# The mixer's front of a decoder layer: its matmuls, vector and scalar work put in a written order, and the branch weights split into parts during the gates

## The chip, the cores and the metric

The kernel runs on one core of a Trainium2 chip. The metric is the device time of one execution in microseconds. A core has a matrix engine (TensorE, PE in the profile), a vector engine (VectorE, DVE), a scalar engine (ScalarE, ACT), a general engine (GpSimd, POOL) and an engine that here only issues transfers (SyncE, SP). Each of them takes its own instructions strictly in order and waits for the others by semaphores.

## The reference

One layer of a decoder trunk, batch 1, 1024 positions of width 1024, all in f32:

```python
x = x + 0.5 * swiglu(rmsnorm(x), ffn1)
z = rmsnorm(x) @ w_in                  # u | v | c_q | c_kv | k_rope | q_mem | three gates
u, v = gelu(z_u), gelu(z_v)
y_a = spatial_gating(u, v)             # u * (tril(W) layernorm(v) + b), chunks of 128, 8 groups
y_b = mla(c_q, c_kv, k_rope)           # 8 heads, causal, latent queries and keys (w_uq, w_ukv)
y_c = memory_attention(q_mem, mem)     # 4 heads of 128, 256 memory tokens, softmax
gates = sigmoid(z_gates + b)
merged = gates_A * (y_a @ w_a) + gates_B * (y_b @ w_b) + gates_C * (y_c @ w_c)
x = x + merged @ w_out
x = x + 0.5 * swiglu(rmsnorm(x), ffn2)
```

## The kernel before, in words

**Products in three passes.** An f32 operand is split into a high part (a cast, on ScalarE, line 134) and a low part (the operand minus the high part, on VectorE, line 135). A product is three matmuls, high by high, low by high and high by low (`mm3`, lines 148 to 150). Weights that are loaded as f32 go through the same split in `convert`.

**Stages.** First feed-forward half; the input projection (class `Gates`: 19 units of output columns, in a product scheme of Strassen's kind, each of some 19 us); the mixer; output projection; second feed-forward half. The projection leaves u (after GELU), the gates and the latent columns in DRAM tiles named gate, and the memory queries as zhi and zlo; the value columns of z (w_v) are left to the mixer.

**The mixer's front** has four pieces of work, all written in `mixer`:

- Value rows: four groups of two chunks of 128 positions (half f = 1 first, then 0), 48 matmuls each, GELU on ScalarE (line 582), the layer norm on VectorE (statistics line 591, centring 593, the reciprocal root in nine small operations 163 to 167, scaling 596), then a split into tiles h.
- Spatial gating (`gating`): mix(f, j) multiplies a quarter of the groups, ScalarE adds the bias (633); out(f, j) transposes the result on TensorE (643), VectorE multiplies by u (644) and the product is split.
- Memory attention (`mem_attention`): scores(t) for eight blocks of 128 positions into one of two PSUM pairs mm; a minimum on VectorE (724), four exponentials on ScalarE (732) into a tile mpr, of which there are four, the division by the sum (736, 737); turn(i) transposes, value(i) multiplies by the memory values.
- Branch steps (`branches`): y_a @ w_a and later y_c @ w_c. A step takes one tile of 128 output channels, a half of 512 positions, 12 matmuls into one bank; a sink on VectorE multiplies by the gate row (937 for A, 943 for C). A's product is stored in DRAM (md); C's sink loads md, GpSimd adds, and the sum is stored (mc).

Four PSUM banks (`bank`), two pairs (`mm`), five tiles each of whi and wlo, three of raw and six rows t are shared by all of it. In the front before, the framework's scheduler chooses the order of the instructions on each engine, with the order of the code as its first guess; `mixer` uses branch A's steps as filler by calling `next` on the generator.

**Behind the front** stand the latent norm, the query and key/value products of the latent attention (`qkv`), and the attention. There `next` on branch C's generator gives filler: two steps in `mixer`, one in each of the eight blocks of `qkv`, and the rest while the attention gets its first operands. These go through DRAM: q and k are normed on VectorE (lines 516 to 525), stored as qd and kd (533, 530), loaded as aq and ak, half 0 and half 1 (`pair_half`, 543) and transposed on TensorE (406).

SP's queue issues nearly all transfers. A transfer whose tile is not yet free holds up all behind it in the queue.

## Time and profile before

| What | Value |
|---|---|
| Time, median of 3 runs | 2188.55 us (2187.59 to 2189.79) |
| Span of the profiled execution | 2187.2 us, which is 1.35 us below that median |
| PE busy | 2163.2 us, 99% |
| DVE, ACT, POOL busy | 1560.4 us (71%), 908.5 us (42%), 219.0 us (10%) |
| Moved by DMA | 315.80 MB, mean 144 GB/s |

The profiled execution is one run with its own time, and only its span is given. The span is the time from the first to the last instruction of that execution; the runs' times are those of whole executions. The granted clock of TensorE is 0.9 or more in all 40 slices. In the rows, a name such as whi or bank is that of a tile in the program, and L135 is line 135.

Places on the span's axis: the gates end at about 1060 us, the front reaches to about 1150, the last key/value product ends at 1256, and the attention's first transposed operands come at 1272.

### The profile page before, as it was taken

What the parts mean: (1) busy time and instruction counts of PE and PEld (TensorE: products, weight loads), DVE (VectorE), ACT (ScalarE), POOL (GpSimd) and SP (SyncE); (2) the same over time, 40 slices, a digit from 0 to 9 for tenths busy, and PEclk for the clock granted to TensorE, in tenths of its full rate; (3) what the DMA queues carried; (4) which work ended last, traced back from release to release, by engine and by line L of the source; (5) the groups of instructions that cost most, each with busy time, mean ns of one, the idle gap of its engine ahead of it and who ended that gap; (6) DMA issues with size and microseconds to landing.
All of it is one profiled execution on the core that took longest, in us unless ns stands there. A gap on an engine that the chain in (4) does not pass through costs nothing.

```text
span 2187.2 us, 27190 instructions
## 1 busy us (share of the span) xinstructions
PE 2163.2 (99%) x10153; PEld 1797.6 (82%) x10153; DVE 1560.4 (71%) x2285; ACT 908.5 (42%) x1375; POOL 219.0 (10%) x234
## 2 busy tenths in 40 slices
PE   8999999999999999999999999999999999999999
PEld 4788888888888888888888889988888888888887
DVE  7965666569889657556588788898985665556964
ACT  5432223233445435433266549844532322224332
POOL 0011212110000220000000431200001111211000
PEclk9999999999999999999999999999999999999999
DMA  4232333384432673334356661166243333338442
GB/s 155 88 124 91 112 101 114 107 329 151 151 125 81 227 260 106 135 135 170 118 173 198 207 202 35 54 229 238 82 135 96 97 115 92 116 130 317 140 140 97
DMA packets 131925, 315.80 MB, mean 144 GB/s; under 512 B 14608, under 2 KB 23056, under 8 KB 131792
## 3 DMA queue, kind: packets, MB, share of 16 engines
q1 hardware_dynamic: 129392, 311.69, 42.6%
q10 hardware_dynamic: 2400, 2.36, 0.3%
q8 instruction: 80, 1.31, 0.3%
q14 instruction: 53, 0.43, 0.1%
HBM read 216.35 MB, written 97.65 MB: 144 GB/s over the span
## 4 chain that ended last, share of the span: by engine, by line
PE 87%; DVE 9%; DMA 2%; ACT 1%; issue 1%; POOL 0%; SPq 0%; ACTq 0%; DVEq 0%; POOLq 0%
PE one L148 15%; PE one L150 15%; PE one L149 15%; PE bank L148 10%; PE bank L149 10%; PE bank L150 10%; PE mm L148 2%; DVE wlo L135 2%; PE mm L150 2%; PE mm L149 2%; PE bank L864 1%; PE bank L879 1%; DVE h L135 1%; PE bank L880 1%; PE bank L406 1%
## 5 line engine op out<-in xcount | busy, mean ns | idle before, releaser
L134 ACT CAST whi<-x 128x1024 fp32r<-128x1024 f32 (+1 forms) x213 | 200.5, 946 | 510.4 <-PE one L149 213.1
L1457 DVE TENSOR_TENSOR t<-t,one 128x512 f32<-128x512 f32 x149 | 102.3, 687 | 245.0 <-PE one L150 244.8
L135 DVE TENSOR_TENSOR wlo<-x,whi 128x1024 fp32r<-128x1024 f32 (+1 forms) x213 | 233.3, 1099 | 42.5 <-ACT whi L134 42.5
L148 PE MATMUL bank<-h,whi 128*128 128x512 f32 x592 | 231.1, 391 | 1.1 <-ACT t L1483 0.7
L149 PE MATMUL bank<-h,whi 128*128 128x512 f32 x592 | 230.5, 389 | 0.0
L150 PE MATMUL bank<-h,wlo 128*128 128x512 f32 x592 | 230.4, 390 | 0.0
L135 DVE TENSOR_TENSOR wlo<-w,whi 128x1024 fp32r<-128x1024 f32 (+1 forms) x153 | 168.8, 1117 | 75.3 <-ACT whi L134 75.1
L134 ACT CAST whi<-w 128x1024 fp32r<-128x1024 f32 (+1 forms) x153 | 142.4, 954 | 167.0 <-PE one L149 104.9
L148 PE MATMUL one<-h,whi 128*128 128x512 f32 x528 | 206.6, 391 | 1.7 <-ACT t L1483 1.2
L150 PE MATMUL one<-h,wlo 128*128 128x512 f32 x528 | 205.6, 389 | 0.5 <-DVE wlo L135 0.5
L149 PE MATMUL one<-h,whi 128*128 128x512 f32 x528 | 205.5, 389 | 0.0
L148 PE MATMUL one<-w,whi 128*128 128x512 f32 x464 | 180.7, 390 | 0.3 <-DVE t L1457 0.3
L150 PE MATMUL one<-w,wlo 128*128 128x512 f32 x464 | 180.6, 389 | 0.0
L1971 POOL TENSOR_TENSOR raw<-raw 128x512 f32<-128x512 f32 x36 | 75.6, 2100 | 882.5 <-DVE raw L1829 652.2
L1457 DVE TENSOR_TENSOR raw<-t,one 128x512 f32<-128x512 f32 x130 | 89.1, 686 | 88.1 <-PE one L150 81.1
L149 PE MATMUL one<-w,whi 128*128 128x512 f32 x380 | 147.9, 389 | 0.0
L148 PE MATMUL one<-whi 128*128 128x512 f32 (+1 forms) x371 | 143.9, 388 | 0.0
L149 PE MATMUL one<-wlo,whi 128*128 128x512 f32 (+1 forms) x371 | 143.7, 387 | 0.0
L150 PE MATMUL one<-whi,wlo 128*128 128x512 f32 (+1 forms) x371 | 143.7, 387 | 0.0
L148 PEld LDWEIGHTS bank<-h,whi 128*128 128x128 f32 x592 | 111.1, 188 | 24.6 <-ACT t L1483 1.2
L150 PEld LDWEIGHTS bank<-h,wlo 128*128 128x128 f32 x592 | 111.1, 188 | 23.2
L149 PEld LDWEIGHTS bank<-h,whi 128*128 128x128 f32 x592 | 111.2, 188 | 22.7
(424 smaller groups left out, 4784.8 us busy)
## 6 DMA issues: line engine op xcount, KB each, us to landing
x<-in_ffn_w_gu_dram SPq DMA_DIRECT2D x76, 512.0 KB, 4.4
w<-tdt SPq DMA_DIRECT2D x40, 512.0 KB, 3.8
tdb<-raw SPq DMA_DIRECT2D x64, 256.0 KB, 2.0
gate<-raw SPq DMA_DIRECT2D x32, 512.0 KB, 3.5
w<-tdb SPq DMA_DIRECT2D x30, 512.0 KB, 6.9
h<-in_ffn_w_down_dram SPq DMA_DIRECT2D x28, 512.0 KB, 6.5
x<-in_w_in_dram SPq DMA_DIRECT2D x26, 512.0 KB, 6.1
tdt<-w SPq DMA_DIRECT2D x44, 256.0 KB, 2.0
```

What stands on the lines that cost most here:

```text
L134: (copy or self.nc.scalar.copy)(hi, src)
L135: return (eng or self.nc.vector).tensor_tensor(lo, src, hi.bitcast(F32), op=ALU.subtract)
L148: mmul(out, s[0], m[0], start=first, stop=False, **kw)
L149: mmul(out, s[0], m[1], start=False, stop=False, **kw)
L150: self.last = mmul(out, s[1], m[0], start=False, stop=last, **kw)
L406: nc.tensor.transpose(b[:m, k * P:(k + 1) * P], s, self.ident)
L864: nc.tensor.transpose(b[:, at:at + P], prs[t][:, kk * P:(kk + 1) * P], self.ident)
L879: nc.tensor.matmul(o, w, pt[0], start=n == 0, stop=False)
L880: nc.tensor.matmul(o, w, pt[1], start=False, stop=n == len(pts) - 1)
L1457: return self.nc.vector.tensor_tensor(out, x, y, op=ALU.add)
L1971: sub = lambda d, x, y: eng.tensor_tensor(d, x, y, op=ALU.subtract)
```

## The change

**Weights as parts.** `Gates` gets a method `part`. In units 9 to 15 it loads 512 KB of a weight that the mixer will want (branch A and C two tiles at a time, three blocks of w_uq, two of w_ukv: 13 parts), splits it as described and stores both halves in DRAM (wparts). It uses the tiles x4 and w4 of the units' own rings. The mixer then loads ready high and low parts: a branch-A tile into one whi or wlo tile, a branch-C tile into one raw tile, the query and key weights into whi and wlo pairs. No split of these weights is left in the mixer, and twice the bytes are loaded there.

**The written order.** The front runs inside `manual_schedule` for PE, DVE and Activation: on these three engines the instructions stand as the code is written. The helpers are cut into smaller functions (`rows`, `gelu`, `center`, `norm`, `put` for the value rows; `scores`, `exps`, `scale`, `turn`, `value` for the memory attention; `mix` and `out` for the gating), and `mixer` calls them one by one. The scores of blocks 0 to 3 stand inside the value rows; before, all of them came behind. All 16 steps of branch A stand in the front (before, 13), six tiles of half 1 first in place of four. The gate rows of branch A have a ring of their own of two tiles, and a sink stands one step later than its matmuls (lag = 1). mpr has six tiles. Exponentials and GELU now alternate on ScalarE.

The diff, cut to what moves (a line of only "..." marks what is left out; the old `value_rows` and `value_norm` did what `values` does):

```diff
-        wq = self.load(a["mla_w_uq"])
-        wk = [self.load(a["mla_w_ukv"][g]) for g in range(2)]
+        def weights(n, width):
+            t = [self.wide(x, F32)[:, :2 * width].rearrange("p (c w) -> p c w", c=2) for x in ("whi", "wlo")]
+            for i, x in enumerate(t):
+                nc.sync.dma_start(x, self.wparts[n][:, i])
+            return [tuple(x[:, c].bitcast(F32R) for x in t) for c in range(2)]
+
+        wq = [x for q in range(QR // P) for x in weights(("q", q), H * QK // 2)]
+        wk = [weights(("k", g), 512) for g in range(2)]
...
+    def branches(self, br, yt, sink, halves, rooms, first=3, row=None, lag=0):
+
+        nc, w, rooms, held = self.nc, {}, list(rooms), []
 
         steps = [(dt, hf) for hf in halves for dt in range(first)]
         for dt, hf in steps + [(dt, hf) for dt in range(first, DT) for hf in halves]:
             if dt not in w:
-                w[dt] = self.load(
-                    a["w_branch"][br, dt], rooms.pop(0) if rooms else None,
-                    copy=nc.vector.tensor_copy if br == 2 and dt >= DT - 2 else None)
-            sig = self.row()
+                t = rooms.pop(0)()
+                nc.sync.dma_start(
+                    t.rearrange("p (a w) -> p a w", a=2), self.wparts[br, dt // 2][:, :, dt % 2])
+                t = t.bitcast(F32R)
+                w[dt] = [
+                    tuple(t[:, x + k * P:x + (k + 1) * P] for x in (0, 512)) for k in range(4)]
+            sig = (row or self.row)()
             nc.sync.dma_start(sig, self.sig[br * DT + dt][:, hf])
             b = self.bank()
             self.branch(b, w[dt], yt, hf)
-            sink(dt, hf, sig, b)
+            held.append((dt, hf, sig, b))
+            if len(held) > lag:
+                sink(*held.pop(0))
             yield
+        for x in held:
+            sink(*x)
...
-            if d in aside:
-                aside[d]()
...
+    def values(self, h, w, ln_g, ln_b, vs):
+
+        v, groups = self.nc.vector, [(1, 0), (1, 1), (0, 0), (0, 1)]
+        bank, x, mv, out = {}, {}, {}, {}
+
+        def rows(n, d0=0, d1=DT):
+            f, q = groups[n]
+            if n not in bank:
+                bank[n] = [self.bank() for _ in range(2)]
+            for d in range(d0, d1):
+                for i, b in enumerate(bank[n]):
+                    c = slice((2 * q + i) * P, (2 * q + i + 1) * P)
+                    self.mm3(b, tuple(y[:, c] for y in h[f][d]), w[d], d == 0, d == DT - 1)
+
+        def gelu(n):
+            x[n] = self.x4()
+            for k in range(2):
+                self.nc.scalar.activation(x[n][:, k], bank[n][k], ACT.Gelu)
...
-            for t in range(4):
-                scores(t)
-                for go in lead[t]:
-                    go()
-                if t == 1:
-                    query(1)
-            yt += [self.split_pair(self.h4) for _ in range(MH)]
-            for i in range(4):
-                turn(i)
-                fill()
-                if i < 2:
-                    scores(2 * i + 4)
-                if i == 3:
-                    fill()
-                value(i)
-                if i < 3:
-                    fill()
-                if i < 2:
-                    scores(2 * i + 5)
-        return filler
+    def mem_attention(self, p, kt, vv, qt, nr, yt):
+
+        nc = self.nc
+        sc, pr, sm, pt = {}, {}, {}, {}
+
+        def scores(t):
+            sc[t] = self.mm().rearrange("p a (b m) -> p (a b) m", b=2)
+            for hh in range(MH):
+                self.mm3(
+                    sc[t][:, hh], tuple(x[:, t % 4 * P:t % 4 * P + P] for x in qt[hh, t // 4]),
+                    tuple(x[:, hh] for x in kt), True, True)
+
+        def exps(t):
+            mx = self.stat("m_mx", MH)
+            nc.vector.tensor_reduce(mx, sc[t], axis=AXX, op=ALU.min)
+            nc.vector.scalar_tensor_tensor(
+                mx, in0=mx, scalar=-1.0, in1=nr[:, t], op0=ALU.mult, op1=ALU.mult)
+            pr[t] = p.tile([P, MH, ML], F32, name="mpr", bufs=6)
+            sm[t] = self.stat("m_sm", MH)
...
+        E = mybir.EngineType
+        with tc.tile_pool(name="mem", bufs=1) as p, tc.manual_schedule(engines={E.PE, E.DVE, E.Activation}):
             w = self.convert(self.w_v)
             kt, vv = self.mem_operands(p)
             qt, nr, query = self.mem_query(p)
             query(0)
-            vs = [[], []]
-            sw = self.gating_weights()
-            ya, aside = self.gating(sw, vs)
-            branch_a = self.branches(0, ya, sink_a, (1, 0), first=4)
-            fill, mix = (lambda x=x: next(x) for x in (branch_a, aside))
-            for f, q, also in ((1, 0, {}), (1, 1, {}), (0, 0, {}), (0, 1, {d: mix for d in (1, 2, 4, 6, 7)})):
-                x = self.value_rows(f, q, h, w, also)
-                self.value_norm(x, q, ln_g, ln_b, vs[f])
-            lead = [(fill, fill), (fill, mix, mix), (mix, fill), (mix, mix, fill)]
-            branch_c = self.mem_attention(
-                kt, vv, qt, nr, query, lead, branch_a, lambda yc: self.branches(
-                    2, yc, sink_c, (0, 1), [self.half_pair] * DT, first=1))
+            vs, yc = [[], []], []
+            ya, mix, out = self.gating(self.gating_weights(), vs)
+            row = lambda: p.tile([P, 512], F32, name="sig", bufs=2)
+            wide = [lambda x=x: self.wide(x, F32) for x in ("whi", "wlo")]
+            branch_a = self.branches(0, ya, sink_a, (1, 0), wide * (DT // 2), first=6, row=row, lag=1)
+            step = lambda: next(branch_a, None)
+            rows, gelu, center, norm, put = self.values(h, w, ln_g, ln_b, vs)
+            scores, exps, scale, turn, value = self.mem_attention(p, kt, vv, qt, nr, yc)
+
+            rows(0)
+            gelu(0)
+            center(0)
+            norm(0)
+            rows(1, 0, 4)
+            scores(0)
+            exps(0)
+            rows(1, 4)
+            gelu(1)
+            scale(0)
+            put(0)
+            scores(1)
+            exps(1)
+            center(1)
+            norm(1)
+            scale(1)
+            rows(2, 0, 4)
+            scores(2)
+            put(1)
+            exps(2)
+            rows(2, 4)
+            scores(3)
+            scale(2)
+            gelu(2)
+            exps(3)
+            center(2)
+            query(1)
+            rows(3, 0, 2)
+            mix(1, 0)
+            rows(3, 2, 3)
+            mix(1, 1)
+            rows(3, 3, 4)
+            out(1, 0)
+            norm(2)
+            mix(1, 2)
+            rows(3, 4, 5)
+            out(1, 1)
+            mix(1, 3)
+            rows(3, 5, 6)
+            put(2)
+            out(1, 2)
+            scale(3)
+            rows(3, 6, 7)
+            out(1, 3)
+            rows(3, 7)
+            gelu(3)
+            scores(4)
+            exps(4)
+            step()
+            center(3)
+            step()
+            norm(3)
+            step()
+            scale(4)
+            put(3)
+            step()
+            mix(0, 0)
+            mix(0, 1)
+            step()
+            out(0, 0)
+            mix(0, 2)
+            step()
+            out(0, 1)
+            mix(0, 3)
+            scores(5)
+            out(0, 2)
+            exps(5)
+            turn(0, 0)
+            out(0, 3)
+            turn(0, 1)
+            scale(5)
+            step()
+            scores(6)
+            exps(6)
+            step()
+            value(0)
+            scale(6)
+            turn(1, 0)
+            turn(1, 1)
+            step()
+            scores(7)
+            exps(7)
+            step()
+            value(1)
+            scale(7)
+            turn(2, 0)
+            turn(2, 1)
+            step()
+            step()
+            value(2)
+            turn(3, 0)
+            turn(3, 1)
+            step()
+            step()
+            value(3)
+            for _ in range(3):
+                step()
+            branch_c = self.branches(2, yc, sink_c, (0, 1), [self.raw] * DT, first=1)
...
+    def part(self, n, src, a, b):
+
+        k, nc = self.k, self.nc
+        a, b = (t()[:, :, :src.shape[-1]] for t in (a, b))
+        nc.sync.dma_start(a, src)
+        hi, lo = b.bitcast(F32R), a.bitcast(F32R)
+        nc.scalar.copy(hi, a)
+        nc.vector.tensor_tensor(lo, a, b, op=ALU.subtract)
+        for i, t in enumerate((b, a)):
+            nc.sync.dma_start(k.wparts[n][:, i], t)
...
+        k.wparts, parts = {}, []
+        for n, src in chain(
+                (((br, q), k.a["w_branch"][br, 2 * q:2 * q + 2].rearrange("c p k w -> p c (k w)"))
+                 for br in (0, 2) for q in range(DT // 2)),
+                ((("q", q), k.a["mla_w_uq"][:, 2 * q:2 * q + 2]) for q in range(QR // P)),
+                ((("k", g), k.a["mla_w_ukv"][g]) for g in range(2))):
+            k.wparts[n] = k.dram.tile([P, 2, *src.shape[1:]], F32, name=f"wp_{n[0]}{n[1]}")
+            parts.append((n, src))
...
+                if f > MEM_AT:
+                    rooms = list(turn[(last - f + 1) % 2])
+                    while parts and rooms:
+                        self.part(*parts.pop(0), rooms.pop(0), rooms.pop(0))
```

Three places in the instructions' order show how it moves them. First TensorE where the attention gets its first operands; ak and aq are the transposed tiles of half 0 and, the second time, of half 1, `bank<-h,raw` a branch-C step, `mm<-x` the first scores. Before:

```order
L150 MATMUL bank<-h_8734,raw 128x512
L148 MATMUL mm<-x_10183,x_10181 128x256
L149 MATMUL mm<-x_10184,x_10181 128x256
L148 MATMUL mm<-x_10183,x_10181 128x256
L149 MATMUL mm<-x_10184,x_10181 128x256
L150 MATMUL mm<-x_10183,x_10182 128x256 x2
L406 MATMUL bank<-ident,ak_10177 96x128 x4
L148 MATMUL bank<-h_8728,raw 128x512
L149 MATMUL bank<-h_8729,raw 128x512
```

After:

```order
L149 MATMUL bank<-h_8981,raw 128x512
L150 MATMUL bank<-h_8980,raw 128x512
L406 MATMUL bank<-ident,aq_10099 96x128 x4
L406 MATMUL bank<-ident,ak_10280 96x128 x4
L148 MATMUL mm<-x_10286,x_10284 128x256
L149 MATMUL mm<-x_10287,x_10284 128x256
L148 MATMUL mm<-x_10286,x_10284 128x256
L149 MATMUL mm<-x_10287,x_10284 128x256
L150 MATMUL mm<-x_10286,x_10285 128x256 x2
L406 MATMUL bank<-ident,aq_10282 96x128 x4
```

Before, a branch-C step stands on either side of the second ak; now the last step is over ahead of aq, and ak follows at once.

Second VectorE where the fourth group of value rows is finished (L596 before, L611 now) and put into the h tiles that mix(0, 0) reads. Before:

```order
L596 SCALAR_TENSOR_TENSOR x_8391<-x_8391,rs_y,t 128x512 x2
L724 TENSOR_REDUCE m_mx<-mm 128x4 x2
L135 TENSOR_TENSOR h_8247<-x_8391,h_8246 128x512
L727 SCALAR_TENSOR_TENSOR m_mx<-m_mx,m_nr 128x4
L135 TENSOR_TENSOR h_8249<-x_8391,h_8248 128x512
L727 SCALAR_TENSOR_TENSOR m_mx<-m_mx,m_nr 128x4
L937 TENSOR_TENSOR t<-t,bank 128x512 x3
L736 RECIPROCAL m_rs<-m_sm 128x4
L737 TENSOR_TENSOR mpr<-mpr,m_rs 128x1024
```

After:

```order
L167 SCALAR_TENSOR_TENSOR rs_y<-rs_b,rs_y 128x2
L611 SCALAR_TENSOR_TENSOR x_8611<-x_8611,rs_y,t 128x512 x2
L922 TENSOR_TENSOR sig<-sig,bank 128x512
L743 RECIPROCAL m_rs<-m_sm 128x4
L744 TENSOR_TENSOR mpr<-mpr,m_rs 128x1024
L135 TENSOR_TENSOR h_8569<-x_8611,h_8568 128x512
L135 TENSOR_TENSOR h_8571<-x_8611,h_8570 128x512
L922 TENSOR_TENSOR sig<-sig,bank 128x512
L141 SCALAR_TENSOR_TENSOR x_9389<-raw,c_mla_cq_norm,x_9388 128x1024
L922 TENSOR_TENSOR sig<-sig,bank 128x512
L662 TENSOR_TENSOR t<-t,bank 128x512
```

The minimum of the scores (L724) no longer stands between; a sink of branch A (L922, before L937) and a division by the sum (L743, L744) now stand ahead of the two L135 rows.

Third SP's queue at the last weights of branch A (wp into whi and wlo) and the query weights (wp_q). After:

```order
L923 DMA md<-sig 128x512
L566 DMA sig<-gate_3245 128x512
L923 DMA md<-sig 128x512
L566 DMA sig<-gate_3246 128x512
L560 DMA whi<-wp_4977 128x2x512
L458 DMA whi<-wp_q_4982 128x768
L458 DMA whi<-wp_q_4983 128x768
L560 DMA wlo<-wp_4977 128x2x512
L458 DMA wlo<-wp_q_4982 128x768
L458 DMA wlo<-wp_q_4983 128x768
L923 DMA md<-sig 128x512 x2
L566 DMA sig<-gate_3246 128x512
```

Before, the query weights (L100) were loaded as they are into raw tiles:

```order
L100 DMA raw<-in_mla_w_uq_dram 128x768
L561 DMA t<-gate_3246 128x512
L100 DMA raw<-in_mla_w_uq_dram 128x768
L561 DMA t<-gate_3247 128x512
L100 DMA raw<-in_mla_w_ukv_dram 128x1024
L938 DMA md<-t 128x512
L100 DMA raw<-in_mla_w_ukv_dram 128x1024
L100 DMA raw<-in_w_branch_dram 128x512
L938 DMA md<-t 128x512
```

Now each store of a sink's product (L923) and each gate row (L566) stands in front of loads of ready parts.

154 lines of the change are left out of this document (55 added, 99 removed).

## The prediction

> **What bounds the kernel now.** I read the busy table first, then busy time by stretches of 50 us, then who waited for whom on TensorE inside the stretches that are not full, and last the chain of waits there.
>
> ```profile
> span 2187.2 us, 27190 instructions
> ...
> PE 2163.2 (99%) x10153; PEld 1797.6 (82%) x10153; DVE 1560.4 (71%) x2285; ACT 908.5 (42%) x1375; POOL 219.0 (10%) x234
> ```
>
> TensorE is idle for 2187.2 − 2163.2 = 24.0 us in all. The change leaves the matmuls as they are, so it can only remove or add idle time on this engine. The stretches show where that lies (columns: window, its length, then busy us and count of PE, PEld, DVE, ACT, POOL, then the granted clock, the DMA share and GB/s):
>
> ```profile
> 850.00:900.00 50.00, 50.00 (x228) 41.41 (x227) 33.24 (x64) 23.51 (x32) 0.00 (x0) 1.00 0.40 142
> ...
> 1100.00:1150.00 50.00, 45.93 (x296) 40.50 (x295) 41.57 (x79) 31.75 (x84) 0.00 (x0) 1.00 0.53 178
> 1150.00:1200.00 50.00, 50.00 (x306) 44.91 (x306) 42.06 (x83) 33.65 (x75) 2.57 (x6) 1.00 0.61 198
> ...
> 1250.00:1300.00 50.00, 47.67 (x249) 40.55 (x248) 37.51 (x71) 17.87 (x38) 23.03 (x27) 1.00 0.78 257
> ```
>
> The changed part loses 4.07 us in the mixer's front (1100 to 1150) and 2.33 us where the attention starts (1250 to 1300); the stretch between is full. The waits of TensorE in 1100 to 1140, and then those in 1270 to 1290 (us in total, times, longest):
>
> ```profile
> PE bank L643 <- ACT t L633: 1.9, 4, 0.6
> PE mm L148 <- ACT mpr L732: 1.8, 3, 1.0
> PE bank L148 <- DVE t L937: 0.3, 1, 0.3
> ```
>
> ```profile
> PE bank L148 <- DVE t L943: 1.1, 1, 1.1
> PE mm L150 <- DVE x L141: 1.0, 1, 1.0
> PE bank L406 <- DMA aq<-qd: 0.2, 1, 0.2
> ```
>
> The front has eight waits: four transposes of the gating product that come too soon after ScalarE wrote it, three score groups that wait for a PSUM pair whose exponentials are not done, one bank. A matmul of 512 columns is shown with 0.39 us though these follow each other every 0.23 (72 of them in the next fence), so a gap costs 0.16 more than it shows: the front loses 4.0 + 8 x 0.16 = 5.3 us, the attention's start 2.3 + 3 x 0.16 = 2.8 us. TensorE's timeline there:
>
> ```profile
> 1256.14 0.39 PE L148 MATMUL bank<-h,raw 128*128 128x512 f32 x1
> ...
> 1272.46 0.60 PE L406 MATMUL bank<-ident,ak 128*96 128x128 f32 x4
> ...
> 1282.58 0.61 PE L406 MATMUL bank<-ident,ak 128*96 128x128 f32 x4 [0.23 <-DMA aq<-qd]
> ...
> 1287.35 0.48 PE L148 MATMUL bank<-h,raw 128*128 128x512 f32 x1
> ```
>
> The last key/value matmul starts 0.23 before 1256.14. From there to 1272.46 lie six steps of branch C, 16.32 / 6 = 2.72 us each. They, two more before 1282.58 and two after it are cover: the attention's second half of keys and queries is still on its way through VectorE and DRAM.
>
> **The front, what goes.** With the written order the scores stand inside the value rows and each out(f, j) stands behind other matmuls, so the reasons of the seven waits on ScalarE are gone: −5.3, between −5.3 and 0.
>
> **The front, what comes.** Prices are the groups of VectorE and ScalarE in 1060 to 1150 (count, busy us, mean ns, idle before):
>
> ```profile
> L737 DVE TENSOR_TENSOR mpr<-mpr,m_rs 128x1024 f32<-128x1024 f32 x6 | 7.3, 1224 | 0.1
> L724 DVE TENSOR_REDUCE m_mx<-mm 128x4 f32<-128x1024 f32 x6 | 7.2, 1221 | 1.5 <-PE mm L150 1.5
> L593 DVE SCALAR_TENSOR_TENSOR x<-x,mv,t 128x512 f32<-128x512 f32 x8 | 5.7, 738 | 0.0
> L596 DVE SCALAR_TENSOR_TENSOR x<-x,rs_y,t 128x512 f32<-128x512 f32 x8 | 5.6, 746 | 0.1
> ...
> L135 DVE TENSOR_TENSOR h<-x,h 128x512 fp32r<-128x512 f32 x8 | 5.4, 686 | 1.0 <-ACT h L134 1.0
> ...
> L591 DVE BATCH_NORM_STATS2 bn<-x 128x6 f32<-128x512 f32 x8 | 5.2, 684 | 1.3 <-ACT x L582 1.3
> L135 DVE TENSOR_TENSOR wlo<-raw,whi 128x512 fp32r<-128x512 f32 x7 | 4.7, 689 | 9.3 <-ACT whi L134 9.3
> L937 DVE TENSOR_TENSOR t<-t,bank 128x512 f32<-128x512 f32 x7 | 4.6, 680 | 1.0 <-PE bank L150 1.0
> ...
> L163 DVE SCALAR_TENSOR_TENSOR rs_b<-rs_y 128x2 f32<-128x2 f32 x12 | 1.9, 159 | 0.3
> ```
>
> First place, mix(0, 0) behind put(3). Between scores(4) and mix(0, 0) TensorE has four branch-A steps, 4 x 2.72 = 10.9 us. VectorE, in its written order, has exps(4) 1.22, center(3) 2 x (0.68 + 0.74) = 2.8, a sink 0.68, norm(3) with nine operations of 0.16 and 2 x 0.75 = 2.9, a sink 0.68, scale(4) 1.22 and put(3) 2 x 0.69 = 1.4: 10.9, and with some seven small operations at the 0.16 of the L163 row 12.0 us. So mix(0, 0) waits some 1.2 us; 0 if the value rows' end lets center(3) begin early, 2.5 if VectorE also waits for ScalarE's GELU. I take 1.2.
>
> Second place, out(1, 1) behind norm(2). Its product stands on VectorE behind norm(2), 2.9 us and small operations, about 3.4. The fourth value rows hold two of the four banks, so out(1, 2) needs the bank that this product frees. TensorE has meanwhile two mixes and two eighths of the value rows, 2 x 6 x 0.23 = 2.8 plus two mixes of six matmuls of half the width, 1.4 (an estimate from 0.23). With the split of out(1, 0), 0.69, in front, VectorE comes about 1.0 us too late; I take 1.0, between 0 and 2.
>
> Third, the ring of gate rows. Each branch-A step loads its row into a ring of two, which is free once the step's product has been stored. SP's transfers in 1060 to 1150 (median us to landing):
>
> ```profile
> t<-gate SPq DMA_DIRECT2D x19, 256.0 KB, 3.2
> ...
> md<-t SPq DMA_DIRECT2D x7, 256.0 KB, 3.5
> ```
>
> A round is 0.68 + 3.5 + 3.2 = 7.4 us for two steps, against 5.44 of TensorE. Where steps stand back to back each falls 1.0 us further behind. The four banks carry about two steps, and the matmuls of the memory attention between the pairs catch up, so over the 16 steps it holds: 16 x 2.72 plus those are over the 8 x 7.4 = 59 us. But SP's queue has the weights of the seventh and eighth weight tile and of the queries behind these stores, so a late round also makes weights late. Nothing in the trace has this ring; bounds are 0 (the rows of 1150 to 1200, where no transfer holds TensorE) and 5.0 (two bursts of 2.5). I take 1.5, nearer to the first.
>
> ScalarE's tables: the new order alternates Exp and GELU, six loads of a table more.
>
> ```profile
> L732 ACT ACT_TABLE_LOAD x1 | 1.3, 1283 | 0.0
> ```
>
> 6 x 1.28 = 7.7 us on an engine that is free for 50 − 31.75 = 18 us in that stretch; nothing on TensorE is next behind a GELU but two of four banks, so 0, and 7.7 if every load were on the path. [...]
>
> **The weights as parts.** The 16 branch tiles lose 16 x 0.69 = 11.0 us of VectorE in the mixer, the query and key tiles some more; VectorE is not what ends TensorE's waits at 1150 to 1250, so 0 there. In the gates 13 parts cost 1.12 each on VectorE, 14.5 us, by this group of the page:
>
> ```profile
> L135 DVE TENSOR_TENSOR wlo<-w,whi 128x1024 fp32r<-128x1024 f32 (+1 forms) x153 | 168.8, 1117 | 75.3 <-ACT whi L134 75.1
> ```
>
> They meet a VectorE that is busy 33.24 of 50 and DMA queues at 0.40 (850 to 900) while TensorE has 50.00 of 50: 0. Without that cover each of the 13 would cost its 1.12; I keep 0 to 2 for queued loads.
>
> **The attention's start.** All 16 branch-A steps now stand in the front; before, three were left for later. So the branch-C steps after the last key/value matmul fall from ten to seven: 3 x 2.72 = 8.2 us of cover is moved to a place that needs less. All seven stand before the transposes of ak1 and none after. The chain that must end there:
>
> ```profile
> 1268.88 0.37 ACTq L530
> 1269.34 6.40 DMA kd<-k
> 1275.99 0.34 ACTq L543
> 1276.37 6.15 DMA aq<-qd
> 1282.58 0.61 PE bank L406 x4
> ```
>
> It takes 1282.58 − 1256.14 = 26.4 us. One weight split leaves VectorE inside it:
>
> ```profile
> 1263.36 0.68 DVE L135 TENSOR_TENSOR raw<-raw 128x512 fp32r<-128x512 f32 x1
> ```
>
> so 25.7. TensorE has 7 x 2.72 + 2 x 0.44 (two transposes) = 19.9. The wait would be 5.8 instead of 2.8: +3.0. On the other side fewer gate, md and mc rows of 256 KB compete with kd and aq (share 0.78):
>
> ```profile
> tdb<-raw SPq DMA_DIRECT2D x64, 256.0 KB, 2.0
> ```
>
> At that rate 384 KB would take 3.0, each of the two transfers 3.2 less, and the wait would vanish: −2.8. The rest of kd, qd, ak and aq is still there, so I stay near the crowded rows: +2.0. Behind ak1 the two steps at 1282.95 and 1287.35 are missing under the first softmax tiles; bounds 0 and 5.4 (both steps uncovered). The transposes and scores that remain fill some; +1.0.
>
> **The sum.** −5.3 + 1.2 + 1.0 + 1.5 + 0 + 0 + 2.0 + 1.0 = +1.4 us. On the profiled span that is 2188.6; the median of the runs, 2188.55, lies 1.35 above the span, so 2189.9 us.
>
> **Rivals.**
>
> 1. The front closes and its cover costs nothing later (a shorter DMA chain, VectorE relieved): −5.3 and no new wait, 2183.2 us. For it: VectorE's 12.0 against 10.9 is close, and the wait at 1282.58 is one on DMA. Against: two places where the order of VectorE itself is late. 0.26.
> 2. The attention's start pays for all the moved cover: 8.2 us in place of 3.0, and the new front waits as above, −5.3 + 3.7 + 8.2 = +6.6, 2195.2 us. For it: before, TensorE waited there with ten steps; it decides once the chain stays over 24 us and the first softmax tiles find nothing beside them. Against: kd and aq meet fewer transfers. 0.17.
> 3. The ring of gate rows or the parts that wait in SP's queue set the pace in the long runs of steps: 5.0 in place of 1.5, +4.9, 2193.5 us. For it 7.4 against 5.44; against it the four banks and the average over 16 steps. 0.07.
> 4. The table loads come onto the path: +1.4 + 7.7, 2197.7 us. For it the alternation of Exp and GELU; against it ScalarE's 18 free us. 0.04.
>
> That the matmuls themselves change is excluded: the order shows one row more of some 9,700 on TensorE.
>
> **How the numbers follow.** The forecast, a small net change, has 0.46. A measurement of this kernel can tell about 0.2%, 4.4 us, from no change (its runs spread over 2.2). Faster 0.26, same 0.46, slower 0.28 (rivals 2 to 4). The likeliest one's own range, with each term between its bounds but not all at one end, is 2185 to 2193; with rival 1 on one side and 2 and 3 on the other 2182 to 2196.5.
>
> **What would show it.** Right: 1100 to 1150 no longer has the seven waits on L633 and L732; single waits of about 1 us remain at the first mix of chunk half 0 and at the third out of half 1; ak1's transposes wait 4 to 6 us for kd or aq; 850 to 1050 stays full. Wrong: waits of the branch steps for weights or for gate rows; idle TensorE in the gates; no wait at ak1, which would make rival 1 true; PE busy time other than 2163 would break the premise.

## The result and the profile after

The changed kernel takes 2251.24 us (2248.72 to 2252.78, four runs) against 2188.53 us (2187.59 to 2189.79, four runs) of the kernel before: a ratio of 1.0285, interval 1.0269 to 1.0300. It is 62.7 us slower. The prediction had 2189.9 us, with a range of 2182.0 to 2196.5, and 0.28 for slower.

The first lines of the page of the changed kernel:

```profile
span 2249.9 us, 27251 instructions
...
PE 2181.7 (97%) x10153; PEld 1811.1 (80%) x10153; DVE 1562.5 (69%) x2270; ACT 915.8 (41%) x1370; POOL 217.1 (10%) x234
```

The span is 62.7 us longer, and these two lines split it. TensorE is idle for 2249.9 − 2181.7 = 68.2 us, before it was 24.0: 44.2 us more waiting. And it is busy for 18.5 us more, with 10153 matmuls as before. So the same matmuls have become slower (a little of it is only how rows are shown: by the prediction's reading each gap costs 0.16 us more than it shows). Busy time by stretches of 50 us shows both in one place (the columns are those of the prediction; the third number from the end is the granted clock, here 1.00 or below):

```profile
850.00:900.00 50.00, 50.00 (x229) 41.50 (x228) 40.31 (x71) 28.91 (x38) 0.00 (x0) 1.00 0.80 291
...
1050.00:1100.00 50.00, 46.69 (x221) 38.83 (x220) 27.71 (x70) 16.86 (x32) 1.09 (x1) 0.97 0.39 139
1100.00:1150.00 50.00, 33.41 (x153) 27.09 (x151) 32.21 (x70) 24.70 (x51) 0.00 (x0) 0.83 0.34 118
1150.00:1200.00 50.00, 33.13 (x175) 28.34 (x176) 28.38 (x45) 22.49 (x51) 0.00 (x0) 0.84 0.32 111
1200.00:1250.00 50.00, 42.90 (x229) 36.99 (x229) 20.79 (x34) 14.21 (x31) 0.00 (x0) 0.88 0.59 195
1250.00:1300.00 50.00, 50.00 (x256) 44.36 (x255) 33.40 (x71) 18.69 (x41) 18.77 (x24) 1.00 0.68 222
1300.00:1350.00 50.00, 44.99 (x215) 38.83 (x214) 31.15 (x59) 13.91 (x28) 22.77 (x27) 0.95 0.80 257
```

The gates are as full as before (850 to 900), although DVE has gone from 33.24 to 40.31 us and the DMA share from 0.40 to 0.80. The front, 1050 to 1250, is idle for 3.31 + 16.59 + 16.87 + 7.10 = 43.9 us, where it was 4.1. The attention's start, now in 1300 to 1350, is idle for 5.0 us, where it was 2.3. In 1150 to 1200 TensorE is busy for 33.13 of 50 us, DVE for 28.38 and ACT for 22.49. No engine is the bound there. All three wait for each other.

TensorE's waits in 1050 to 1360 (us in total, times, longest):

```profile
PE bank L771 <- DVE wlo L135: 18.3, 4, 7.1
PE bank L148 <- ACT t L651: 13.8, 8, 3.9
PE bank L148 <- ACT x L597: 6.5, 1, 6.5
PE bank L406 <- DMA ak<-kd: 5.0, 1, 5.0
PE bank L148 <- ACT whi L134: 3.1, 1, 3.1
PE bank L149 <- DVE h L135: 1.2, 1, 1.2
```

None of the kinds of the front before is among the large ones. The transposes of the gating product no longer wait for their ACT pass (L633 before), and no score group waits for exponentials. New kinds took their places, with other prices. Three of them can be followed in the trace.

**The transposes of turn (L771), 18.3 us.** This is the chain of waits around the second of them (start us, us, what):

```profile
1187.24 0.23 PE bank L150
...
1190.22 0.14 PE mm L150
1190.36 0.02 issue
1190.38 0.38 ACT h L134
1190.76 0.02 issue
1190.78 0.44 DVE h L135
...
1193.37 0.42 DVE h L135
...
1193.92 1.22 DVE mpr L744
1195.14 0.61 DVE wlo L135
1195.75 0.04 issue
1195.80 1.11 PE bank L771 x4
1196.91 0.43 PE bank L148
```

value(0) ends at 1190.3. Its result is cast by ACT and split by DVE four times, each after the other, 3.4 us; then comes scale(6) on DVE, 1.22; and only then the low part of turn(1, 0), whose bank the transposes of turn(1, 1) need. On DVE the order is that of the code: value(0), scale(6), turn(1, 0). On TensorE no step stands between. The transposes need nothing of value(0) or scale(6), only a bank that is emptied behind them.

**The halves of a mix (L651), 13.8 us in eight waits.** The second half of a mix writes the bank whose first half ACT has not yet read, and it stands right behind the first. ACT's own order decides how long that takes; ScalarE's timeline at the first mix:

```profile
1107.05 0.57 ACT L737 ACTIVATE mpr<-mm,m_mx,m_nr 128x256 f32<-128x256 f32 x1
1107.72 1.28 ACT L597 ACT_TABLE_LOAD   x1
1109.02 1.08 ACT L597 ACTIVATE x<-bank 128x512 f32<-128x512 f32 x2
1110.59 1.28 ACT L737 ACT_TABLE_LOAD   x1 [0.48 <-DVE m_mx L732]
1111.88 0.56 ACT L737 ACTIVATE mpr<-mm,m_mx,m_nr 128x256 f32<-128x256 f32 x1
...
1114.06 0.48 ACT L651 ACTIVATE t<-bank,c_sg_b 128x256 f32<-128x256 f32 x1
```

The first half ended near 1110.5; its bias pass stands behind a table load and four exponentials of block 3, which nothing needs for another 20 us. The second half starts at 1114.59.

**The first mix itself (L597), 6.5 us,** waits for a bank that GELU of the third group frees, and GELU starts only at 1109.02. GELU stands behind block 2's exponentials, these behind the minimum, and that on DVE behind norm(1), the division of block 1 and put(1).

**The matmuls at half rate.** In the chain of turn above the last row is a matmul of 512 columns: 0.43 us, where the first row, before the wait, has 0.23. TensorE's timeline after the third and the fourth wait of turn:

```profile
1214.28 0.66 PE L771 MATMUL bank<-ident,mpr 128*128 128x128 f32 x4 [4.14 <-DVE wlo L135]
1214.87 0.71 PE L148 MATMUL bank<-h,whi 128*128 128x512 f32 x1
1215.38 0.63 PE L149 MATMUL bank<-h,whi 128*128 128x512 f32 x1
...
1217.94 0.61 PE L149 MATMUL bank<-h,whi 128*128 128x512 f32 x1
1218.37 0.41 PE L150 MATMUL bank<-h,whi 128*128 128x512 f32 x1
1218.62 0.39 PE L148 MATMUL bank<-x,whi 128*128 128x512 f32 x1
...
1229.35 1.11 PE L771 MATMUL bank<-ident,mpr 128*128 128x128 f32 x4 [2.95 <-DVE wlo L135]
...
1234.95 0.63 PE L150 MATMUL bank<-x,whi 128*128 128x512 f32 x1
1235.38 0.44 PE L148 MATMUL bank<-h,whi 128*128 128x512 f32 x1
1235.65 0.39 PE L149 MATMUL bank<-h,whi 128*128 128x512 f32 x1
```

After the wait of 4.14 us the matmuls follow each other every 0.43 us until 1218.4, then every 0.23 again. That is some 4 us at half rate, and 1.8 us lost on top of the wait. After the shorter wait of 2.95 us the half rate holds for 6 us, until 1235.4, and some 3 us are lost; the granted clock of 1230 to 1235 is 0.50. Most of the 18.5 us of additional busy time are such stretches: nine of them between 1068 and 1352, each with a granted clock of 0.50, hold 36.3 us of busy time, of which half, 18.1 us, would be gone at the full rate (an estimate from 0.50 against 1.00).

### The profile page after: what moved, and what is told of

It is laid out like the page before. It is cut to its first block, busy times and chain, and to the rows that moved or that the text cites. A ratio compares the mean times of both kernels' runs of the same rounds, so it can differ in the third digit from the quotient of the medians.

```text
span 2249.9 us, 27251 instructions
## 1 busy us (share of the span) xinstructions
PE 2181.7 (97%) x10153; PEld 1811.1 (80%) x10153; DVE 1562.5 (69%) x2270; ACT 915.8 (41%) x1370; POOL 217.1 (10%) x234
## 4 chain that ended last, share of the span: by engine, by line
PE 83%; DVE 10%; ACT 2%; DMA 2%; issue 2%; SPq 0%; POOL 0%; ACTq 0%; DVEq 0%; POOLq 0%
PE one L148 15%; PE one L150 15%; PE one L149 15%; PE bank L148 10%; PE bank L149 10%; PE bank L150 10%; DVE wlo L135 2%; PE mm L148 1%; PE mm L150 1%; PE mm L149 1%; DVE h L135 1%; PE bank L849 1%; PE bank L864 1%; PE bank L865 1%; PE bank L406 1%
## 5 line engine op out<-in xcount | busy, mean ns | idle before, releaser
L135 DVE TENSOR_TENSOR wlo<-x,whi 128x1024 fp32r<-128x1024 f32 (+1 forms) x213 | 232.5, 1096 | 44.9 <-ACT whi L134 44.3
L135 DVE TENSOR_TENSOR wlo<-w,whi 128x1024 fp32r<-128x1024 f32 (+1 forms) x153 | 168.6, 1116 | 74.6 <-ACT whi L134 74.6
L148 PE MATMUL bank<-h,whi 128*128 128x512 f32 x552 | 218.7, 396 | 1.7 <-ACT t L1564 1.7
L149 PE MATMUL bank<-h,whi 128*128 128x512 f32 x552 | 217.7, 394 | 0.0
L150 PE MATMUL bank<-h,wlo 128*128 128x512 f32 x552 | 214.6, 389 | 0.0
L148 PEld LDWEIGHTS bank<-h,whi 128*128 128x128 f32 x552 | 105.6, 191 | 24.2 <-ACT t L1564 2.1
L149 PEld LDWEIGHTS bank<-h,whi 128*128 128x128 f32 x552 | 105.4, 191 | 21.7
L149 PE MATMUL one<-x,whi 128*128 128x512 f32 x312 | 121.4, 389 | 0.0
```

What stands on the lines that cost most here:

```text
L135: return (eng or self.nc.vector).tensor_tensor(lo, src, hi.bitcast(F32), op=ALU.subtract)
L148: mmul(out, s[0], m[0], start=first, stop=False, **kw)
L149: mmul(out, s[0], m[1], start=False, stop=False, **kw)
L150: self.last = mmul(out, s[1], m[0], start=False, stop=last, **kw)
```

## The experiments

Theory A, formed on these lines: the cost is the order itself. On three engines whose order is written, an instruction that has to wait holds up others that do not, and the chain ACT, DVE, ACT, DVE of a block is not filled by the work of another. Theory B: the parts, with their loads in SP's queue and the ring of two gate rows, set the pace. The rivals of the prediction (table loads, moved cover, the ring) are tested beside them. Most runs are single. Where a run is single, its time stands beside a single run or the median of the kernel before on the same chip (2188.9 to 2191.8 in all).

### The order left to the framework

```diff
-        with tc.tile_pool(name="mem", bufs=1) as p, tc.manual_schedule(engines={E.PE, E.DVE, E.Activation}):
+        with tc.tile_pool(name="mem", bufs=1) as p:
```

> The changed kernel without manual_schedule around the front: the framework orders PE, DVE and ACT there as it did before; the parts, the ring of two gate rows, lag, six mpr tiles and all calls stay. Theory A (the written order itself couples the engines: an instruction that must wait holds up those behind it): most of the 62.7 us goes, 2188 to 2198 us, and the granted clock of 1100 to 1250 is back at 1.00 (0.83 to 0.88 in the changed kernel). Theory B (the parts, their loads in SP's queue and the ring of two gate rows set the pace): it stays above 2235 us.

2220.7 us: 30.6 us less. The four waits on L135 and those of the mix's second halves are gone or small; of the large ones these are left:

```profile
PE bank L406 <- DMA ak<-kd: 6.2, 1, 6.2
PE bank L661 <- ACT t L651: 5.7, 3, 4.9
PE bank L148 <- DMA whi<-wp: 3.8, 1, 3.8
PE mm L148 <- ACT mpr L737: 3.5, 1, 3.5
```

The time lies between what the two theories expected, and the granted clock of 1100 to 1250 (0.86, 0.88, 0.95) is only partly back. Neither theory is right alone. Half the loss is the fixing of the order on the three engines. The other half stays when the framework is free, and it is not yet named.

### The order on TensorE alone

```diff
-tc.manual_schedule(engines={E.PE, E.DVE, E.Activation})
+tc.manual_schedule(engines={E.PE})
```

> The written order for PE alone, the framework orders DVE and ACT. Theory A in the form that the waits come from the order on DVE and ACT (exponentials, casts and splits that stand in front of what TensorE waits for): 2195 to 2215 us, the four waits of the memory attention's transposes on L135 (18.3 us) shrink below 6. Theory A in the form that the order on PE is at fault (halves of a mix side by side, transposes straight behind value): above 2230 us. Theory B: unchanged, about 2250.

2233.9 us, 17.4 less than the changed kernel and 13.2 more than without any written order. The waits of turn on L135, 18.3 us, are not among those above 1.8 us any more; those of the mix's second halves on L651 are still there, 10.4 us in eight, since TensorE's order holds the halves side by side. The time is in the range expected for an order on TensorE at fault, while the waits on L135 went as expected for DVE and ACT. Taken away one after the other, the order on DVE and ACT gives back some 17 us, then that on TensorE some 13.

### No reloads

```diff
-                self.nc.scalar.activation(x[n][:, k], bank[n][k], ACT.Gelu)
+                self.nc.scalar.activation(x[n][:, k], bank[n][k], ACT.Identity)
```

> GELU of the value rows replaced by the identity, which leaves GELU out of the value columns and with it the alternation of tables: five of the six table loads of the front go, 1.28 us each. If the loads are on the path through DVE and ACT (rival 4): 6 to 9 us less, 2242 to 2245 us. If they lie in time that ACT has free: within 2 us of 2251.

2248.2 us, 3.0 less; the runs of the changed kernel spread over 4.1. The wait for the first mix falls from 6.5 to 2.9 us, so the loads are on the path at that place, and at most a part of the 7.7 us shows in the time. The time is in neither of the two expected ranges. Rival 4 explains some 3 us of the 62.7, no more than the runs' spread.

### A step between value and the next turn

```diff
             value(0)
+            step()
             scale(6)
             turn(1, 0)
             turn(1, 1)
-            step()
             scores(7)
```

and the same behind value(1), value(2).

> Five of the branch-A steps moved in the written order from before a value(i) to right behind it, so that one stands between value(i) and the transposes of turn(i+1). Theory A says that the three waits of 4.1, 4.1 and 3.0 us of these transposes (banks held by splits that stand behind the four splits of value(i) on DVE) fall to under 1 each, and the matmuls at half rate behind them (about 2 us each) go too: 14 to 18 us less, 2233 to 2237 us. Theory B: no change, since bytes, rings and queues are the same.

2242.1 us, 9.2 less, where 14 to 18 was expected. The waits in question:

```profile
PE bank L771 <- DVE wlo L135: 9.7, 3, 7.1
PE bank L406 <- DMA ak<-kd: 6.7, 1, 6.7
...
PE bank L771 <- DVE sig L922: 1.5, 3, 0.5
```

Without the 7.1 of turn(0), which was not touched, 2.6 + 1.5 us are left of 11.2. That is theory A at work: same bytes, same instructions, and only three calls written elsewhere (two steps and value(2); the expectation speaks of five steps). The rest of what was expected came back in part at the attention's start, 6.7 in place of 5.0.

### The parts alone

The kernel before with `part` in the gates, the loads of ready halves in `branches` and `qkv`, and nothing else of the change.

```diff
-                w[dt] = self.load(
-                    a["w_branch"][br, dt], rooms.pop(0) if rooms else None, ...)
+                t = rooms.pop(0)()
+                nc.sync.dma_start(
+                    t.rearrange("p (a w) -> p a w", a=2), self.wparts[br, dt // 2][:, :, dt % 2])
```

> The kernel before, its front ordered by the framework, with only the weights as parts: the 13 parts in the gates and the loads of ready high and low halves; gate rows, mpr, the order of the calls and the three branch-A steps left for later stay as before. Theory A: the parts are neutral, 2184 to 2193 us, and the wait on whi<-wp that the run without written order showed (3.8 us) came from where its steps stand. Theory B: part of the remaining 31 us of that run is the parts': 2196 us or more, with waits of the branch steps on whi<-wp or wlo<-wp and idle PE behind 1100.

2197.8 us in a single run, 8.0 more than the kernel before (2189.8, three runs within 1.5) and just in the range of theory B. The gates stay full, and no branch step waits for whi<-wp or wlo<-wp. The loss is in the front, in waits of the old kinds that have grown (3.0 and 2.8 us, before 1.8 and 1.9) and a new one on h:

```profile
PE mm L148 <- ACT mpr L741: 3.0, 3, 2.2
PE bank L652 <- ACT t L642: 2.8, 4, 1.5
PE mm L148 <- DVE h L135: 1.8, 1, 1.8
PE bank L406 <- DMA aq<-qd: 1.7, 1, 1.7
```

Taking 16 casts and splits off ACT and DVE did not make the front shorter. Theory B names the size but not the mechanism. Why the framework's order comes out worse without that work was not tried.

### Three steps left for later

```diff
-            for _ in range(3):
-                step()
-            branch_c = self.branches(2, yc, sink_c, (0, 1), [self.raw] * DT, first=1)
+            branch_c = chain(branch_a, self.branches(2, yc, sink_c, (0, 1), [self.raw] * DT, first=1))
```

> The changed kernel with the last three branch-A steps left for later, as before the change: ten in place of seven steps stand as cover in front of the attention's ak of half 1 and behind. If the moved cover costs what the prediction said and matmuls run at half rate after a long wait: the 5.0 us wait on ak<-kd falls to 0 to 3 us, its slow matmuls (about 2 us) go, and the front does not get longer, 5 to 9 us less, 2242 to 2246. If the chain through DRAM gets later by the same amount: no change, 2249 to 2252.

2249.4 us, 1.8 less, within the spread. The 5.0 us wait on ak<-kd is gone, but waits of 1.6 and 1.9 us with other releasers at the same place took over, and the front's waits stayed. The same edit on the kernel without the written order was clear:

> The changed kernel without the written order (2220.7 us) and with the last three branch-A steps left for later. If the 31 us that remained there without the written order hold the price of the moved cover: the 6.2 us wait on ak<-kd and its slow matmuls go, 5 to 9 us less, 2212 to 2216 us. If the three steps are missed in the front instead: 2218 us or more.

2213.9 us, 6.8 less than with the steps moved. The 6.2 us wait falls to 2.1 + 1.8. So the moved cover costs some 7 us by these two single runs where the order is not written; with the written order it shows in the wait, and 1.8 us in the time.

### The ring of gate rows

```diff
-            row = lambda: p.tile([P, 512], F32, name="sig", bufs=2)
+            row = lambda: p.tile([P, 512], F32, name="sig", bufs=4)
```

> The changed kernel with four gate rows for branch A in place of two (and five mpr tiles in place of six, for room); order and parts as in the changed kernel. Rival 3 of the prediction (a round of store and load, 7.4 us for two steps, paces the runs of steps): 5 us or more off, below 2246. Theory A (the steps are late for other reasons, so the gate rows are there in time): within 2 us of 2251.

2253.5 us: no gain. In the changed kernel DVE waited for a gate row twice in 1050 to 1260, 3.6 us in all; with four rows these waits are gone and the time is not shorter. As for the other half of rival 3, the changed kernel's list has no wait of TensorE for whi<-wp or wlo<-wp. Rival 3 is out. The counterpart without the written order starts from the run with three steps left (2213.9):

> The same, and branch A's gate rows from the common ring of six, each sink right behind its step, as before the change; six steps of half 1 first, six mpr tiles, the parts and the new order of the calls stay. If the small ring and the late sink hold up the framework's order (waits on sig<-gate and on L922): 4 us or more below the run with three steps left. If not, the rest against the parts alone (2197.8 us) lies in the order in which the calls are written, which the framework takes as its first guess: within 3 us of that run.

2220.1 us, 6.2 more than with the ring of its own. This was neither of the outcomes that I had written down: the small ring and the late sink do not hurt the framework's order, if anything they help (two single runs). Against the parts alone (2197.8) the run with three steps left (2213.9) is 16 us longer (14 with each set against its own run of the kernel before), and what differs is the order of the calls, six steps of half 1 first, the ring, the late sink, and the number of mpr tiles. The ring and the sink are not the cause. Which of the others is was not tried on this kernel.

### Two other written orders

The second order takes the waits above one by one. Its beginning and one place of it:

```diff
-            rows(0)
+            rows(0, 0, 2)
+            rows(1, 0, 2)
+            rows(0, 2)
             gelu(0)
-            center(0)
-            norm(0)
-            rows(1, 0, 4)
             scores(0)
+            rows(1, 2, 5)
+            center(0)
             exps(0)
+            norm(0)
...
+            rows(3, 0, 1)
+            mix(1, 0, 0)
+            rows(3, 1, 2)
+            mix(1, 0, 1)
```

> Another written order for the same three engines, made from the waits of the changed kernel: other matmuls between the two halves of each mix, the minimum and the exponentials ahead of the norm and the division behind it, the gating weights' split behind the first value rows, GELU of groups 2 and 3 next to each other, value's splits a step away from the next transposes, three branch-A steps left for later, four gate rows and five mpr tiles. Theory A (which instructions stand in front of a waiting one is the cost, not that the order is written): 2188 to 2205 us, fewer than five waits over 1 us in 1050 to 1250 and the granted clock above 0.95 there. If a written order as such costs (no freedom to take what is ready): above 2225.

2219.3 us, ratio 1.0136, interval 1.0106 to 1.0165: these are against the kernel before. It is 32 us less than the changed kernel, by another order of the same calls; the three steps left for later and the four gate rows, which it has too, gave nothing clear by themselves (−1.8 and +2.3 us). Theory A's expectation of 2188 to 2205 is missed, and so is the other's of above 2225. So this written order does as well as the framework does from the calls of the change (2220.7). Its busy times show where it worked:

```profile
1050.00:1100.00 50.00, 49.47 (x246) 41.55 (x245) 33.92 (x81) 21.96 (x40) 1.28 (x1) 1.00 0.54 192
1100.00:1150.00 50.00, 39.16 (x210) 32.43 (x210) 33.40 (x70) 24.08 (x57) 0.00 (x0) 0.94 0.39 133
1150.00:1200.00 50.00, 36.12 (x215) 31.84 (x214) 33.78 (x55) 25.30 (x60) 0.00 (x0) 0.86 0.35 114
```

The first 50 us are full. Of the 24.7 us idle in the next 100, 17.6 are two waits of my own making: value(0) for a PSUM pair (5.5) and one transpose for a bank (12.1), since block 4's exponentials, which free the pair, stood too late, and block 5's stood on ACT and DVE in front of the split that frees the bank. The third order moves both to an earlier place:

```diff
-            scores(5)
+            exps(4)
...
+            scores(5)
...
-            exps(5)
             turn(1, 0)
```

> The second written order (2219.3 us) with its two large waits taken away by order alone: the exponentials of block 4 ahead of the scores of block 5, so that value(0) finds a free PSUM pair (5.5 us), and the exponentials of block 5 ahead of the transposes of turn(1) (12.1 us), a step between the two parts of turn(1). Theory A: both waits go with the slow matmuls behind them, 2196 to 2206 us. If the latent norm's casts and products, which the framework sets between those of the front on ACT and DVE, hold the engines wherever they come: one wait of over 4 us in 1140 to 1200 stays, 2207 to 2216 us.

2220.8 us, ratio 1.0144, interval 1.0123 to 1.0164: no gain, and in neither of the expected ranges. The two waits are gone and others stand there, 7.9 us on a low part and 6.4 us on two bias passes.

### The latent stage behind the front

In the trace the latent stage's squares, sums and gains (L353, L358, L138, L141) run inside the front. manual_schedule fixes the order of the front's instructions among themselves, and the framework sets others between.

```diff
+        written = ExitStack()
+        written.enter_context(tc.manual_schedule(engines={E.PE, E.DVE, E.Activation}))
...
                 z = self.latent()
+                written.close()
```

> The changed kernel with the written order drawn out over the latent stage, so that its squares (L353), sums (L358) and gains (L138, L141), which the framework had set between the front's instructions on ACT and DVE, stand behind all of the front. If these foreign instructions are what holds up turn(0, 1) (7.1 us) and mix (0, 2) and (0, 3): that wait falls to under 2 us, 8 to 11 us less with the slow matmuls, but the latent stage now has its DMA and its 12 us of casts uncovered in front of the query products: 2243 to 2252. If the front's own order is the cause: the 7.1 stays and the latent stage comes on top, 2255 to 2265.

2266.8 us, 15.6 more. The longest wait of turn falls only from 7.1 to 5.6 us, and a new one comes: the latent stage, now uncovered.

```profile
PE bank L771 <- DVE wlo L135: 16.9, 4, 5.6
...
PE bank L426 <- DVE t L358: 11.8, 1, 11.8
```

> The same for the third written order (2220.8 us). If the foreign instructions hold it: the 7.9 and 3.0 us waits at 1150 to 1163 go, the latent stage is partly uncovered in exchange (three branch-A and two branch-C steps lie there, 13.6 us): 2204 to 2214 us. If not: 2220 or more.

2227.1 us, ratio 1.0173, interval 1.0143 to 1.0202: 6.3 more than the third order. Its 7.9 us falls to 4.4, and 9.5 us come on L358. By these waits the foreign instructions cost some 2 to 4 us where they stand, and save some 10 us by standing there.

### Six mpr tiles in the kernel before

```diff
-                pr = p.tile([P, MH, ML], F32, name="mpr", bufs=4)
+                pr = p.tile([P, MH, ML], F32, name="mpr", bufs=6)
```

> The kernel before with six tiles for the exponentials (mpr) in place of four and nothing else. The page showed three waits of the score groups on ScalarE's exponentials, 1.8 us in all. If they are waits for a tile of that ring (the exponentials of a block start late because its tile is not free): 1 to 3 us faster, 2186 to 2188. If they are waits for the PSUM pair that the exponentials read, as the row's names say: no change.

2192.0 us, ratio 1.0013, interval 1.0003 to 1.0023. It is not faster, and slightly slower. With six tiles the three waits on the exponentials are still there, 1.9 us in all (before 1.8). They were waits for the pair, as their rows name it, and not for a tile of the ring. No version that was run beats the kernel before.

## Why the prediction was wrong

- **What bounds the kernel.** TensorE does, and the work of the matmuls was left as it was; but "PE busy time other than 2163 would break the premise", and it is 2181.7. The premise that the change "can only remove or add idle time" failed by 18.5 us: behind waits such as those of 4.14 and 2.95 us the matmuls also came more slowly, 0.43 in place of 0.23 us for a row of 512 columns.
- **The front, what goes (−5.3).** Right in kind. The waits that it named are not among the new large ones.
- **The front, what comes (+1.2 +1.0).** This is the step that failed. It priced two places in an order of some ninety calls, and priced each by the sum of DVE's work against TensorE's. The measured front is idle 39.8 us more. At the first place, mix(0, 0), the waits were there (1.2 on the low parts, then its second halves), so this term was right. At the second the third out did not wait; the lateness of norm(2) showed at the second half of mix(1, 3), 2.9 us instead of 1.0, whose bank ACT read only after the split of out(1, 1), and that stood on DVE behind norm(2). The large ones were never looked at: the second half of each mix behind the bias pass of the first, GELU behind exponentials, and turn's splits behind value's. Each is seen by asking, for every matmul with a bank to wait for, what stands ahead on ACT and on DVE of the instruction that frees it. A sum of busy time cannot show them: DVE has as much to do as before (1562.5 us in all, before 1560.4), and in 1150 to 1200 it is busy for only 28.38 of 50 us.
- **The ring of gate rows (+1.5).** 7.4 against 5.44 us looked like a bound; four rows in place of two gave no gain. The term was too large, and with it rival 3.
- **The tables (0).** Six loads more came, at 1.28 us, and the next activation started 0.01 to 0.02 us behind each of the seven in 1060 to 1150. At one place they lengthen a wait by 3.6 us; in the time the loads' removal gave 3.0.
- **The parts (0).** Right for the gates, which are as full as before. Wrong for the mixer, where the parts alone cost 8.0 us (one run); by which mechanism is open.
- **The attention's start (+2.0 +1.0).** The wait at ak was put at 5.8 us, of which I took a part off for the emptier queue. With that, 2.8 + 2.0 = 4.8 was forecast and 5.0 measured, so the size was right. The reason for the discount was not: the transfers of kd and ak took 6.37 and 5.77 us, about the 6.40 and 6.15 of before, in a queue as full (share 0.80, before 0.78). So it is luck that the size came out. The +1.0 behind ak1 was not measured by itself. The price of rival 2, 8.2 us, is near the 6.8 that leaving the three steps behind gave back without the written order; with it they gave 1.8.

Most of the signs on record came true: the old waits gone, 1.2 us at the first mix of half 0, 5.0 us at ak1, full gates. The time was 61 us off all the same, since the signs looked only at the places that had been priced.

By their sizes: order on three engines 30.6 us (without manual_schedule), of it some 17 on DVE and ACT; parts 8.0; moved cover 6.8. The last two were measured in other surroundings than the change, so they need not add up with the first; the rest, some 14 to 17 us that may lie in the order of the calls, the first six steps or the mpr tiles, is open. So the written order is shown as the cause of half the loss, and the waits of turn behind value(i) by moving three calls. The waits of the mixes' second halves fall from 13.8 to 0.4 us in the second order, which puts other matmuls between the halves but changes more besides; the chain at GELU is read from the trace.

## What to carry to other kernels

A written order over several engines is a promise about every wait in it. Before you trust one, take each matmul that needs a bank, find the instruction that frees it on ACT or DVE, and read what stands ahead of that instruction and what those wait for; a framework that may reorder can hide such chains, and then their cost doesn't show in the trace of before. And where TensorE sets the pace, look at the matmuls behind a wait too: here those behind a wait of 2.95 us cost some 3 us more.

## What the hardware showed that was not expected

TensorE ran at half rate after long waits: rows of 512 columns follow each other at 0.43 in place of 0.23 us, for some 4 us behind the wait of 4.14 us that ends at 1214.28 and for 6 us behind that of 2.95 us, and the granted clock of the three 50 us stretches in 1100 to 1250 reads 0.83, 0.84 and 0.88. The length of the wait alone did not decide it. In the changed kernel a wait of 2.37 us was followed by full rate at once (rows every 0.23 us from 1125.03 on, granted clock 1.00 in 1124.5 to 1127.5), and the next one, 2.86 us, by rows every 0.43 us until 1133. The longest, 7.10 us, was followed by 2.7 us of half rate, less than the 6 us behind the wait of 2.95 us; and behind three waits of 1.21, 0.62 and 0.62 us within 1149.5 to 1153.6 the rows came every 0.43 us until 1156.9. Without the table reloads the four waits of turn are as long as in the changed kernel (18.3 us, the longest 7.1), and the granted clock of 1200 to 1250 reads 0.97 in place of 0.88. What decides whether and for how long the rate falls is not shown. Priced by these rows, the waits of 4.14 and 2.95 us would have stood 1.8 and some 3 us higher in a forecast; that would not have found the waits.

The table load took 1.28 us each of the seven times in 1060 to 1150; the next activation started 0.01 to 0.02 us behind it (at one of them 1107.72 + 1.28 = 1109.00, then 1109.02).
